# SBUF pools laid out so that the operands of every 512-column product start at multiples of 256 bytes

## Chip, cores and metric

The kernel runs on one core of a Trainium2 chip. The metric is the device time of one execution in microseconds (us); the time stated for a kernel is the median of its runs. TensorE's granted clock is given as a share of full speed: 1.00 is 2.4 GHz, 0.50 is 1.2 GHz.

## What is computed

One layer of a hybrid backbone over 2,048 latent tokens of width 1,024, with a prefix of 256 context tokens:

```
proj = rms_norm(x) * (1 + scale) + shift  @  w_in        # 2048 x 1024 @ 1024 x 5632, 11 slots of 512 channels
A: bidirectional gated recurrence (RG-LRU)      B: short gated convolution
C: GLU -> conv31 -> LayerNorm -> swish -> 512x512 product      D: 2-D box means minus the token
cat  = [ya*silu(za), yb*silu(zb), yc*silu(zc), yd*silu(zd)]        # 2048 x 2048
out  = rms_norm(x + gate * (cat @ w_out))                          # 2048 x 2048 @ 2048 x 1024
```

## The kernel before, in words

**The products.** Every float32 operand is split into a high and a low part (`split`, L104 to L107), and a product is three TensorE products into one PSUM bank: high by high, high by low, low by high. Almost all of TensorE's work is such products with a stationary operand (weights) of 128x128 and a moving operand of 128x512. The weights of each product are loaded anew (the profile's engine PEld), while the product before it still streams.

- The input projection (`project`, L331, its products at L339; `project_two`, L347, its products at L356): the moving operand is `hb`, the prepared tokens (four tiles of 32 KB per partition, pool `big`), the weights are `wh` and `wl` (pool `wp`), in two jobs also `whl` (pool `acc`). One `project` call is 2 x 8 x 3 x 2 = 96 products.
- The gates of group A (`lru_block`, L408): moving `xh`, `xl` (pool `lru`), weights `gwh`, `gwl` (pool `sm`).
- The pointwise product of group C (`finish_c`, L811): moving `uh`, `ul` (pool `mid`), weights `pw` (pool `lru`).
- The output projection (L992): a block scheme of seven 512-column products for each pair of token tiles, in the order 1, 2, 6, 7, 4, 5, 3. The moving operand is `wo` (pool `big`), the weights are `ahl` (pool `mid`, three buffers that take turns). 56 groups (7 blocks by 8 tiles) of 24 products each.
- Two smaller kinds with 256 columns: the modulation (`modulation_pair`, L226: moving `modwhl`, weights of only four columns) and the context's projection (`context`, L633: moving `hc`, weights `wh`, `wl`).

**The order.** The string `JOBS` (L37) orders the projections, mixers and gates by hand; within it a scheduler places each engine's instructions by priority. Evacuations of PSUM run at raised priority. Loads go through SP's queue, stores mostly through POOL's.

**Where tiles lie.** Pools lie one behind the other in SBUF in the order in which they are opened (L52 to L61): `const`, `big` (4 buffers), `mid` (3), `wst` (2), `wp` (3 for each of two tags), `lru` (4), `acc` (1), `zp` (3), `bp` (2), `sm`. A tag's buffer is as large as its largest tile, and each tile is rounded up to 32 bytes. All these are per partition. The compiled kernel before has these start addresses in bytes, and remainders by 256:

| tile (pool) | start of each buffer | remainder by 256 |
|---|---|---|
| `ident`, `onesm` (const) | 16,512; 17,024 | 128; 128 |
| `schl` (const) | 18,752 | 64 |
| `hb`, `wo`, `modwhl` (big) | 19,904 + 32,768 n | 192 |
| `ahl`, `uh`, `ul`, `hc` (mid) | 150,976; 159,296; 167,616 | 192; 64; 192 |
| `wh`, `wl` (wp) | 180,032 + 2,048 n | 64 |
| `xh`, `xl`, `pw` (lru) | 192,320 + 4,096 n | 64 |
| `whl`, `hl` (acc) | 208,704 | 64 |
| `gwh`, `gwl` (sm) | 223,776; 225,824 | 32 |

A mid buffer is 8,320 bytes because of its largest tile, `vc` (L492: two planes of 1,040 values); 8,320 is 32.5 x 256, so every second buffer has the other remainder. Within a tile the products' slices are steps of 512 or 2,048 bytes and change no remainder.

Of the kernel before, what the change touches and what calls it, by code (L numbers as in the profile page):

```python
# [8 lines left out]
F32 = mybir.dt.float32  # L9
F32R = mybir.dt.float32r  # L10
# [4 lines left out]
P = 128  # L15
T = 2048
# [3 lines left out]
NK = D // P  # L20
# [4 lines left out]
WINS = (2, 4, 8, 16)  # L25
# [19 lines left out]
def flow_backbone_kernel(  # L45
# [4 lines left out]
    nc = tc.nc  # L50
    PSUM = bass.MemoryType.PSUM
    const = ctx.enter_context(tc.tile_pool(name="const", bufs=1))  # L52
# [5 lines left out]
    acc_p = ctx.enter_context(tc.tile_pool(name="acc", bufs=1))  # L58
    zp = ctx.enter_context(tc.tile_pool(name="zp", bufs=3))
    bp = ctx.enter_context(tc.tile_pool(name="bp", bufs=2))  # L60
    sm = ctx.enter_context(tc.tile_pool(name="sm", bufs=2))  # L61
    dram = ctx.enter_context(tc.tile_pool(name="dram", bufs=1, space=bass.MemoryType.DRAM))
    pm = ctx.enter_context(tc.tile_pool(name="pm", bufs=4, space=PSUM))
# [17 lines left out]
    def z2(name, shape=(P, 512)):  # L81
        return zp.tile(list(shape), F32, tag="z2", name=name)

    def b2(name):
        return bp.tile([P, 512], F32, tag="b2", name=name)

    def mid_t(name, shape, dt=F32):
        return mid.tile(list(shape), dt, tag="mid", name=name)
# [7 lines left out]
    def gate_ps(name):  # L96
        return pg.tile([P, 512], F32, tag="pg", name=name)
# [6 lines left out]
    def split(hi, lo, src, sub=None):  # L104

        nc.scalar.activation(hi, src, AF.Copy)  # L106
        (sub or nc.vector).tensor_tensor(lo, src, hi.bitcast(F32), op=SUB)  # L107


    rows1 = z2("rows1", shape=(R_EARLY, W))  # L110
    for eng, r, n, src in (
        (nc.scalar, R_C, 2, c.rearrange("b (h w) -> (b h) w", w=W)),
# [27 lines left out]
        for kk in range(1, 4):  # L140
            load_modw(kk)

    ident = const.tile([P, P], F32, name="ident")
    with tc.high_priority(offset=3 * URGENT):
        make_identity(nc, ident)
    onesm = const.tile([P, P], F32R, name="onesm")
    nc.scalar.activation(onesm, ident, AF.Copy, bias=1.0 / W, scale=0.0)
    fixed = const.tile([P, 4], F32, name="fixed")
    ones2, eps_rms, eps_ln = fixed[:, 0:2], fixed[:, 2:3], fixed[:, 3:4]
# [1 line left out]
        nc.vector.memset(t, v)  # L151


    lacks = const.tile([P, sum(w // 2 for w in WINS)], F32, name="lacks")
    lack = []
    for w in WINS:
        at = sum(v // 2 for v in WINS if v < w)
# [7 lines left out]
    def par(r, q):  # L165
        return pt[:, q, r : r + 1]
# [210 lines left out]
        return gw  # L377

    def split_gate_weights(q):
        gh = sm.tile([P, 4, P], F32R, tag="gwh", name="gwh", bufs=1)  # L380
        gl = sm.tile([P, 4, P], F32R, tag="gwl", name="gwl", bufs=1)
        split(gh, gl, gate_weights(q))
        return gh, gl

# [101 lines left out]

    HP = T // 2 + 16

    def c_slots(q):
        v = mid_t("vc", (P, 2, HP))  # L492
        nc.gpsimd.memset(v[:, :, 0:8], 0.0)
        nc.gpsimd.memset(v[:, :, HP - 8 : HP], 0.0)

        def planes(b, ps):
            return v[:, :, 8 + 256 * b : 8 + 256 * (b + 1)], ps.rearrange("p (m e) -> p e m", e=2)

        def ev_g(b, ps):
            s, src = planes(b, ps)  # L500
            nc.scalar.activation(s, src, AF.Sigmoid)

        def ev_a(b, ps):
            s, src = planes(b, ps)
            nc.vector.tensor_tensor(s, src, s, op=MUL)

        return v, ev_g, ev_a

    def c_conv31(v, q):
        n = T // 2  # L510
        x1, x0 = v[:, 0, :], v[:, 1, :]
        even, odd = (lambda j: par(R_CCONV + 2 * j, q)), (lambda j: par(R_CCONV + 2 * j + 1, q))
        bb = aux["pool"].tile([P, n], F32, tag="conv", name="cb")
        nc.vector.tensor_scalar(bb, x1[:, 1 : 1 + n], odd(0), None, op0=MUL)
        for j in range(1, 15):
            nc.vector.scalar_tensor_tensor(bb, x1[:, 1 + j : 1 + j + n], odd(j), bb, op0=MUL, op1=ADD)  # L516

        nc.vector.tensor_tensor(x1, x1, x0, op=ADD)
        acc = acc_p.tile([P, n], F32, tag="acc", name="cacc")
        nc.vector.tensor_scalar(acc, x0[:, 0:n], even(0), None, op0=MUL)  # L520
        for j in range(1, 16):
            nc.vector.scalar_tensor_tensor(acc, x0[:, j : j + n], even(j), acc, op0=MUL, op1=ADD)  # L522

        end = sm.tile([P, 17], F32, tag="cend", name="cend", bufs=1)
        nc.vector.scalar_tensor_tensor(
            end[:, 1:17], x0[:, n : n + 16], 1.0, pt[:, q, R_CCONV : R_CCONV + 31 : 2], op0=MUL, op1=MUL, accum_out=end[:, 0:1]
        )

        nc.vector.tensor_tensor(x0[:, 0:n], acc, bb, op=ADD)
        nc.gpsimd.dma_start(u_d[q][:, 0, :], x0[:, 0:n])  # L530
        nc.vector.scalar_tensor_tensor(acc[:, : n - 1], x1[:, 1:n], csum[:, q, 0:1], acc[:, 1:n], op0=MUL, op1=SUB)
        nc.vector.scalar_tensor_tensor(
            acc[:, n - 1 : n], x1[:, n : n + 1], csum[:, q, 0:1], end[:, 0:1], op0=MUL, op1=SUB
        )
        for j in range(1, 16):
            nc.vector.scalar_tensor_tensor(acc, x1[:, 1 + j : 1 + j + n], csum[:, q, j : j + 1], acc, op0=MUL, op1=ADD)  # L536
        nc.vector.tensor_tensor(acc, acc, bb, op=SUB)
        nc.gpsimd.dma_start(u_d[q][:, 1, :], acc)
# [159 lines left out]
    def group_d(q):  # L698
        h = WINS[q] // 2
        g = mid_t("gd", (P, GR, GW))  # L700
        gf = g.rearrange("p r c -> p (r c)")

        def evac(b, ps):
            s = slice(512 * b, 512 * (b + 1))
            nc.scalar.activation(gf[:, s], ps, AF.Copy)
            if b % 2 == 1:
                s = slice(512 * (b - 1), 512 * (b + 1))
                nc.gpsimd.dma_start(dv_d[q][b // 2], gf[:, s])

        project(DV, q, evac)  # L710
        dw = sm.tile([P, P], F32, tag="dw", name="dw", bufs=1)
        nc.gpsimd.dma_start(dw, d_w[0, q])

        for rows, n in ((False, GW), (True, GR)):

            def cut(t, lo, hi):

                return t.rearrange("p r c -> p (r c)")[:, lo * GW : hi * GW] if rows else t[:, :, lo:hi]

            def back(t):  # L720

                return t[:, ::-1] if rows else t[:, :, ::-1]

            if h > 1:
                pre = acc_p.tile([P, h - 1, GW] if rows else [P, GR, h - 1], F32, tag="acc", name="pre")
                nc.vector.tensor_copy(cut(pre, 0, h - 1), cut(g, 0, h - 1))
                k = 1
                while k < h - 1:
                    upper = back(cut(pre, k, h - 1))
                    nc.vector.tensor_tensor(upper, upper, back(cut(pre, 0, h - 1 - k)), op=ADD)  # L730
                    k *= 2
            k = 1
            while k < h:
                nc.vector.tensor_tensor(cut(g, 0, n - k), cut(g, 0, n - k), cut(g, k, n), op=ADD)
                k *= 2
            upper = back(cut(g, h, n))
            nc.vector.tensor_tensor(upper, upper, back(cut(g, 0, n - h)), op=ADD)
            if h > 1:
                nc.vector.tensor_tensor(cut(g, 1, h), cut(g, 1, h), cut(pre, 0, h - 1), op=ADD)

            for lo, hi, f in ((0, h, lack[q]), (n - h + 1, n, lack[q][:, :0:-1])):
                if hi > lo:
                    m = hi - lo
                    ff = f.unsqueeze(2).broadcast_to([P, m, GW]) if rows else f.unsqueeze(1).broadcast_to([P, GR, m])
                    e = g[:, lo:hi, :] if rows else g[:, :, lo:hi]
                    nc.vector.tensor_tensor(e, e, ff, op=MUL)
        dbs = sm.tile([P, 1], F32, tag="dbs", name="dbs")
        nc.vector.tensor_tensor(dbs, par(R_DB, q), par(R_DSC, q), op=MUL)
        for b in range(NB):
            o, s = 512 * (b % 2), gf[:, 512 * b : 512 * (b + 1)]  # L750
            dv = b2("dvr")
            nc.sync.dma_start(dv, dv_d[q][b // 2][:, o : o + 512])
            nc.vector.scalar_tensor_tensor(s, s, 1.0 / (4 * h * h), dv, op0=MUL, op1=SUB)
            ps = gate_ps("dps")
            nc.tensor.matmul(ps, lhsT=dw, rhs=s, start=True, stop=True)  # L755
            nc.scalar.activation(s, ps, AF.Identity, bias=dbs, scale=par(R_DSC, q))
            nc.gpsimd.dma_start(y_d["d", q][b // 2][:, o : o + 512], s)
# [73 lines left out]


    def gate_mod(e):
        acc = sm.tile([P, P], F32, tag="macc", name="macc", bufs=1)
        mod_tile(2, e, 0, acc, [b2("mws").rearrange("p (k e) -> p k e", e=P) for _ in range(2)])
        mod_sums(2, e, 1, 0, acc)

# [22 lines left out]
    gcol = sm.tile([P, NK], F32, tag="gcol", name="gcol", bufs=1)  # L860
    nc.vector.tensor_copy(gcol, mod[:, 2, :, 0])
    nc.tensor.transpose(gps[:NK, :P], gcol, ident)
    grow = sm.tile([NK, P], F32, tag="grow", name="grow", bufs=1)
    nc.vector.tensor_copy(grow, gps[:NK, :P])
    gd = dram.tile([NK, P], F32, name="gd", tag="gd")
    nc.sync.dma_start(gd, grow)
# [183 lines left out]
```

## Time and profile before

| | |
|---|---|
| median of 3 runs | 1,550.73 us (1,548.19 to 1,552.17) |
| the profiled execution: its time | 1,551.9 us |
| the profiled execution: its span, first to last instruction | 1,549.8 us |
| granted clock of TensorE over the span | 0.985 |
| busy share: TensorE products, weight loads | 95%, 77% |
| busy share: VectorE, ScalarE, GpSimd | 72%, 43%, 11% |
| share of the chain that ended last: TensorE, "issue", DMA | 64%, 18%, 10% |

Busy time is a share of the span. Successive products overlap in the trace (one is shown as lasting some 390 ns, the next starts some 230 ns after it), so the distance between the starts of two products, here called the cadence, says what a product costs, not the duration shown.

### The profile page before, as it was taken

How to read it: one execution, taken by the hardware profiler on the slowest of the kernel's cores; microseconds unless marked ns; L12 is line 12 of the kernel's file. 1: busy time of each engine (PE TensorE's matmuls, PEld its weight loads, DVE VectorE, ACT ScalarE, POOL GpSimd, SP SyncE). 2: the span in 40 equal slices, each digit the busy share in tenths (PEclk: the TensorE clock that was granted, in tenths of full speed). 3: DMA queues.
4: the chain of work that ended last, by engine and by line, in shares of the span. 5: the costliest groups of instructions: out<-in, count | busy, mean ns of one | idle time of the engine just before them, and what ended most of it. 6: DMA issues, size and time to landing. Idle time of an engine off the chain costs nothing.

```text
span 1549.8 us, 17881 instructions
## 1 busy us (share of the span) xinstructions
PE 1479.4 (95%) x6457; PEld 1186.2 (77%) x6457; DVE 1117.4 (72%) x1573; ACT 662.4 (43%) x949; POOL 166.4 (11%) x290
## 2 busy tenths in 40 slices
PE   5999999999999999999999999979999699999997
PEld 3778888887788888788877887857877487788886
DVE  6889984859956898988754875554646446765897
ACT  7773475543144541244635435322424332433432
POOL 0200000100100000111011001313222210000000
PEclk9999999999999999999999999989999799999999
DMA  9412121322311223233253126557466977775674
GB/s 341 143 51 87 42 92 49 106 83 69 110 38 37 86 75 109 86 109 122 82 161 110 63 75 218 180 170 221 155 225 205 332 221 253 254 232 170 214 250 150
DMA packets 157308, 223.88 MB, mean 144 GB/s; under 512 B 16283, under 2 KB 98211, under 8 KB 157220
## 3 DMA queue, kind: packets, MB, share of 16 engines
q1 hardware_dynamic: 135836, 154.29, 31.4%
q0 software_dynamic: 19648, 65.31, 12.0%
q10 hardware_dynamic: 1736, 3.15, 0.7%
q8 instruction: 50, 0.82, 0.2%
q14 instruction: 38, 0.31, 0.1%
HBM read 149.29 MB, written 73.40 MB: 144 GB/s over the span
## 4 chain that ended last, share of the span: by engine, by line
PE 64%; issue 18%; DMA 10%; POOL 3%; DVE 3%; SPq 1%; ACT 1%; POOLq 0%; DVEq 0%; ACTq 0%
PE ps L339 45%; PE q L992 12%; PE gps L408 3%; PE ps L356 3%; DMA yp<-first 2%; DMA sums<-yp 1%; POOL sums L456 1%; DMA yt<-yb 1%; SPq L126 1%; DMA sums<-yt 1%; DMA wos<-in_w_out_dram 1%; DMA ws<-in_w_in_dram 1%; PE dps L755 1%; PE psc L633 1%; POOL second L452 1%
## 5 line engine op out<-in xcount | busy, mean ns | idle before, releaser
L339 PE MATMUL ps<-hb,wh 128*128 128x512 f32 x2560 | 730.1, 399 | 10.3 <-ACT sz L464 9.6
L339 PEld LDWEIGHTS ps<-hb,wh 128*128 128x128 f32 x2560 | 483.4, 189 | 131.4 <-ACT sz L464 11.4
L339 PE MATMUL ps<-hb,wl 128*128 128x512 f32 x1280 | 418.1, 398 | 0.0
L992 PE MATMUL q<-wo,ahl 128*128 128x512 f32 x1344 | 312.1, 394 | 14.2 <-ACT sz L464 10.1
L992 PEld LDWEIGHTS q<-wo,ahl 128*128 128x128 f32 x1344 | 253.4, 189 | 72.9 <-ACT sz L464 10.6
L339 PEld LDWEIGHTS ps<-hb,wl 128*128 128x128 f32 x1280 | 241.9, 189 | 58.8 <-issue 1.7
L106 ACT ACTIVATE wh<-ws 128x512 fp32r<-128x512 f32 x94 | 58.7, 627 | 174.3 <-PE ps L339 153.1
L470 DVE TENSOR_TENSOR sz<-sz,yt 128x512 f32<-128x512 f32 x48 | 32.9, 685 | 92.6 <-DMA yt<-yd 30.5
L107 DVE TENSOR_TENSOR wl<-ws,wh 128x512 fp32r<-128x512 f32 x91 | 62.1, 684 | 33.1 <-ACT wh L106 32.9
L464 ACT ACTIVATE sz<-ps 128x512 f32<-128x512 f32 x64 | 36.7, 595 | 102.3 <-DMA second<-sz 34.2
L536 DVE SCALAR_TENSOR_TENSOR cacc<-vc,csum,cacc 128x1024 f32<-128x1024 f32 x60 | 76.7, 1278 | 0.3
L522 DVE SCALAR_TENSOR_TENSOR cacc<-vc,pt,cacc 128x1024 f32<-128x1024 f32 x60 | 76.6, 1276 | 0.0
L414 ACT ACTIVATE gate<-gps,pt 128x512 f32<-128x512 f32 x64 | 40.9, 686 | 83.3 <-PE gps L408 83.2
L516 DVE SCALAR_TENSOR_TENSOR cb<-vc,pt,cb 128x1024 f32<-128x1024 f32 x56 | 71.7, 1281 | 0.0
L356 PE MATMUL ps<-hb,wh 128*128 128x512 f32 x192 | 65.6, 413 | 5.7 <-ACT sz L464 4.7
L106 ACT ACTIVATE wo<-wos 128x512 fp32r<-128x512 f32 x56 | 34.5, 628 | 74.4 <-DVE wos L910 42.5
L394 DVE SCALAR_TENSOR_TENSOR xc<-va,pt,xc 128x1024 f32<-128x1024 f32 x48 | 61.3, 1278 | 0.2
L423 DVE SCALAR_TENSOR_TENSOR xc<-xc,gate 128x1024 f32<-128x1024 f32 x16 | 19.6, 1224 | 44.5 <-ACT xc L422 44.5
L910 DVE TENSOR_TENSOR wos<-wos,wot 128x512 f32<-128x512 f32 x40 | 27.0, 689 | 33.8 <-DMA wos<-in_w_out_dram 18.4
L107 DVE TENSOR_TENSOR wo<-wos,wo 128x512 fp32r<-128x512 f32 x56 | 37.5, 687 | 18.1 <-ACT wo L106 17.4
L106 ACT ACTIVATE ahl<-s 128x1024 fp32r<-128x1024 f32 x32 | 33.5, 1054 | 36.4 <-PE q L992 32.9
L356 PEld LDWEIGHTS ps<-hb,wh 128*128 128x128 f32 x192 | 36.6, 194 | 15.3 <-ACT sz L464 5.9
(255 smaller groups left out, 1876.1 us busy)
## 6 DMA issues: line engine op xcount, KB each, us to landing
ws<-in_w_in_dram SPq DMA_DIRECT2D x96, 256.0 KB
s<-sums SPq DMA_DIRECT2D x32, 512.0 KB
wos<-in_w_out_dram SPq DMA_DIRECT2D x40, 256.0 KB
wot<-in_w_out_dram SPq DMA_DIRECT2D x40, 256.0 KB
modw<-in_mod_w_dram SPq DMA_DIRECT2D x8, 1024.0 KB
a<-second SPq DMA_DIRECT2D x16, 512.0 KB
xo<-in_x_dram SPq DMA_DIRECT2D x32, 256.0 KB
out_dram<-ys SPq DMA_DIRECT2D x32, 256.0 KB
```

Of the source, the lines that this page charges most:

```text
L106: nc.scalar.activation(hi, src, AF.Copy)
L107: (sub or nc.vector).tensor_tensor(lo, src, hi.bitcast(F32), op=SUB)
L339: nc.tensor.matmul(ps[u], lhsT=wk, rhs=hb[2 * pr + u][:, k, part, :], start=(k == 0 and n == 0), stop=(k == NK - 1 and n == 2),)
L356: nc.tensor.matmul(ps, lhsT=wk, rhs=hb[b][:, k, part, :], start=(k == 0 and n == 0), stop=(k == NK - 1 and n == 2),)
L394: nc.vector.scalar_tensor_tensor(xc, v[:, o + k : o + k + n], par(w0 + k, q), xc, op0=MUL, op1=ADD)
L408: nc.tensor.matmul(ps, lhsT=w[:, 2 * d + g, :], rhs=xx[:, u : u + m], start=(i == 0), stop=(i == len(terms) - 1))
L414: nc.scalar.activation(dst[:, u : u + m], ps, AF.Sigmoid, bias=par(bias, q))
L464: nc.scalar.activation(sz, ps, AF.Silu)
L516: nc.vector.scalar_tensor_tensor(bb, x1[:, 1 + j : 1 + j + n], odd(j), bb, op0=MUL, op1=ADD)
L522: nc.vector.scalar_tensor_tensor(acc, x0[:, j : j + n], even(j), acc, op0=MUL, op1=ADD)
L536: nc.vector.scalar_tensor_tensor(acc, x1[:, 1 + j : 1 + j + n], csum[:, q, j : j + 1], acc, op0=MUL, op1=ADD)
L992: nc.tensor.matmul(ps, lhsT=hl[:, a, k, :], rhs=wo[:, k, w, :], start=(k == 0 and e == 0), stop=(k == NK - 1 and e == 2))
```

## The change

The instructions and their order in the source stay; tiles move. (1) `lacks`, `ident` and `onesm` become the first tiles of `const`, and `lacks` grows from 15 to 32 values. (2) A new pool `gp` behind `bp` takes `gwh`, `gwl`, `dw`, and a tile `row` that serves both `macc` (in `gate_mod`) and, later, `grow`; they leave `sm`. (3) The two planes of `vc` grow from 1,040 to 1,056 values, which makes a mid buffer 8,448 bytes; the same eight values at each end are set to zero, and `c_conv31` works on the first 1,040.

```diff
@@ flow_backbone_kernel
+    gp = ctx.enter_context(tc.tile_pool(name="gp", bufs=1))
...
+    lacks = const.tile([P, 32], F32, name="lacks")
+    ident = const.tile([P, P], F32, name="ident")
+    onesm = const.tile([P, P], F32R, name="onesm")
...
-    ident = const.tile([P, P], F32, name="ident")
...
-    onesm = const.tile([P, P], F32R, name="onesm")
...
-    lacks = const.tile([P, sum(w // 2 for w in WINS)], F32, name="lacks")
@@ split_gate_weights
-        gh = sm.tile([P, 4, P], F32R, tag="gwh", name="gwh", bufs=1)
-        gl = sm.tile([P, 4, P], F32R, tag="gwl", name="gwl", bufs=1)
+        gh = gp.tile([P, 4, P], F32R, tag="gwh", name="gwh")
+        gl = gp.tile([P, 4, P], F32R, tag="gwl", name="gwl")
@@ c_slots
-    HP = T // 2 + 16
+    HP = T // 2 + 32
...
-        nc.gpsimd.memset(v[:, :, HP - 8 : HP], 0.0)
+        nc.gpsimd.memset(v[:, :, 8 + T // 2 : 16 + T // 2], 0.0)
@@ c_conv31
-        x1, x0 = v[:, 0, :], v[:, 1, :]
+        x1, x0 = v[:, 0, : n + 16], v[:, 1, : n + 16]
@@ group_d
-        dw = sm.tile([P, P], F32, tag="dw", name="dw", bufs=1)
+        dw = gp.tile([P, P], F32, tag="dw", name="dw")
@@ gate_mod
-        acc = sm.tile([P, P], F32, tag="macc", name="macc", bufs=1)
+        acc = gp.tile([P, P], F32, tag="row", name="macc")
@@ before the output projection
-    grow = sm.tile([NK, P], F32, tag="grow", name="grow", bufs=1)
+    grow = gp.tile([NK, P], F32, tag="row", name="grow")
```

## Rows read from the trace of the kernel before

**Rows 1.** The page's part 1: busy us, share of the span, instructions of each engine.

```profile
PE 1479.4 (95%) x6457; PEld 1186.2 (77%) x6457; DVE 1117.4 (72%) x1573; ACT 662.4 (43%) x949; POOL 166.4 (11%) x290
```

**Rows 2.** Busy time by stretch: length, each engine's busy us, clock, DMA share, GB/s.

```profile
127.00:1005.00 878.00, 877.31 (x3753) 704.00 (x3753) 673.36 (x849) 384.44 (x491) 83.12 (x157) 1.00 0.29 94
1005.00:1236.00 231.00, 200.02 (x799) 156.46 (x798) 123.84 (x197) 76.75 (x111) 58.66 (x81) 0.93 0.66 217
1236.00:1530.00 294.00, 290.63 (x1264) 236.57 (x1263) 205.81 (x306) 106.64 (x174) 11.34 (x18) 1.00 0.70 226
```

**Rows 3.** The chain that ended last, pieces at L339: start, length, products.

```profile
135.55 48.10 PE ps L339 x207
...
569.73 35.92 PE ps L339 x154
```

**Rows 4.** Busy time at L992 alone, four successive groups: length, PE, PEld, clock, DMA.

```profile
1244.32:1249.76 5.44, 5.44 (x25) 4.50 (x24) 1.00 0.43 112
1249.76:1255.35 5.59, 5.59 (x25) 4.52 (x24) 1.00 0.72 234
1255.35:1260.81 5.46, 5.46 (x26) 4.50 (x25) 1.00 0.81 239
1260.81:1266.25 5.44, 5.44 (x25) 4.50 (x24) 1.00 0.59 183
```

**Rows 5.** Groups by line and shape, TensorE: count, busy us, mean ns, idle before.

```profile
L339 PE MATMUL ps<-hb,wh 128*128 128x512 f32 x2560 | 730.1, 399 | 10.3 <-ACT sz L464 9.6 <-ACT vb L679 0.7
L339 PE MATMUL ps<-hb,wl 128*128 128x512 f32 x1280 | 418.1, 398 | 0.0
L992 PE MATMUL q<-wo,ahl 128*128 128x512 f32 x1344 | 312.1, 394 | 14.2 <-ACT sz L464 10.1 <-DVE ahl L107 3.1 <-ACT ys L998 0.7
L356 PE MATMUL ps<-hb,wh 128*128 128x512 f32 x192 | 65.6, 413 | 5.7 <-ACT sz L464 4.7 <-DVE hb L107 0.8
L811 PE MATMUL pwps<-uh,pw 128*128 128x512 f32 x128 | 41.1, 395 | 1.3 <-ACT uh L106 1.3
...
L408 PE MATMUL gps<-xl,gwh 128*128 128x512 f32 x64 | 25.3, 395 | 0.0
```

**Rows 6.** Busy time at L339 alone over the second stage: length, PE, PEld.

```profile
127.00:1005.00 878.00, 819.86 (x3428) 643.88 (x3429) 1.00 0.29 94
```

**Rows 7.** Timeline of PE at L339 while the granted clock was 0.50.

```profile
1020.00 1.05 PE L339 MATMUL ps<-hb,wh 128*128 128x512 f32 x2
1020.86 0.63 PE L339 MATMUL ps<-hb,wl 128*128 128x512 f32 x1
1021.28 1.05 PE L339 MATMUL ps<-hb,wh 128*128 128x512 f32 x2
```

**Rows 8.** Timeline of PE at L633, 256 columns, granted clock 1.00.

```profile
120.18 0.40 PE L633 MATMUL psc<-hc,wh 128*128 128x256 f32 x2
120.42 0.28 PE L633 MATMUL psc<-hc,wl 128*128 128x256 f32 x1
120.54 0.40 PE L633 MATMUL psc<-hc,wh 128*128 128x256 f32 x2
```

**Rows 9.** Busy time at L226 alone, 256 columns: length, PE, PEld, clock, DMA.

```profile
17.77:19.47 1.70, 1.70 (x17) 1.26 (x15) 1.00 1.09 348
```

**Rows 10.** Timeline of DVE, the low part of `ahl` in two successive buffers.

```profile
1404.56 1.23 DVE L107 TENSOR_TENSOR ahl<-a,ahl 128x1024 fp32r<-128x1024 f32 x1 [0.41 <-ACT ahl L106]
...
1410.15 1.23 DVE L107 TENSOR_TENSOR ahl<-a,ahl 128x1024 fp32r<-128x1024 f32 x1 [0.41 <-ACT ahl L106]
```

**Rows 11.** Busy time by stretch, all engines, the start and the fullest stretch of DVE.

```profile
0.00:50.00 50.00, 30.01 (x212) 21.52 (x213) 33.62 (x63) 37.53 (x65) 9.97 (x29) 1.00 0.89 299
500.00:600.00 100.00, 100.00 (x431) 80.48 (x430) 92.61 (x86) 45.60 (x55) 7.84 (x18) 1.00 0.24 79
```

**Rows 12.** The tiles `macc` and `grow`: durations min/median/max, first and last start.

```profile
L206 PE MATMUL modps<-fixed,macc x16: 165/210/251, 232.1 to 648.0; 128*128 128x2 f32 x16
...
L864 DVE COPY grow<-gateT x1: 272/272/272, 1202.1 to 1202.1; 8x128 f32<-8x128 f32 x1
```

## The prediction

> **What bounds the kernel.** The page's busy shares come first: TensorE is busy in 95% of the span and its weight loads in 77%, VectorE in 72% [rows 1]. The busy times by stretch say where that matters. From 127 to 1,005 us TensorE is busy in 877.3 of 878 us, so what its products cost is what the stage costs. From 1,005 to 1,236 it is busy in 200 of 231 and waits for others in between. From 1,236 to 1,530 it is busy in 290.6 of 294 [rows 2]. So for two stages of 1,172 us together the question is what one product costs.
>
> The chain of waits answers that for the input projection: 48.10 us for 207 products and 35.92 us for 154, together 84.02 us for 361, a cadence of 232.7 ns [rows 3]. The reader is to set beside this the output projection, where a group is 24 products of the same shape: 5.44 us (226.7 ns each), 5.59 us (232.9 ns), 5.46 us (227.5 ns), 5.44 us [rows 4]. The clock is 1.00 in all, the moving tile `wo` is the same, nothing waits (PE is busy throughout). What differs is the buffer of the weights. `ahl` takes the three mid buffers in turn, and the slow group is the one whose weights start at remainder 64 by 256; the others start at 192, as `wo` does. The input projection has weights at 64 and a moving operand at 192 throughout, and the cadence of the slow group. So the trace holds both cases: weights and moving operand at equal remainders, 226.7 ns; 128 bytes apart, 232.7 to 232.9.
>
> **What the change does to the addresses.** With `lacks` 128 bytes and first, `ident` starts at 16,640 = 65 x 256 and `onesm` at 17,152 = 67 x 256; the 32-byte roundings of the other tiles of `const` end it at 19,968 = 78 x 256, where `big` starts. `big` is 512 x 256 bytes, so `mid` starts at 151,040 = 590 x 256; its buffers are now 33 x 256, so all three have remainder 0. Everything behind them up to `gp` comes in multiples of 256. `gwh` and `gwl`, the only others, lie in `gp` and no longer in `sm`. So all operands of the 512-column products have remainder 0, equal for both. Remainder 0 itself occurs nowhere in the trace of before.
>
> **The sum, part by part.** A product that goes from unequal to equal remainders saves 232.7 - 226.7 = 6.0 ns, if 0 beside 0 does what 192 beside 192 does. I take that value because it is the only row with 512 columns and equal remainders. The products are 3,840 at L339, 1,344 at L992, 192 at L356 with two like rows of 96 beside it (384), 128 at L811 with 64 more (192), 64 at L408 with two like rows (192) [rows 5].
>
> - 127 to 1,005 us: 3,428 products of L339 [rows 6], all 192 of L408 and 48 of L811, 3,668 x 6.0 ns = 22.0 us. TensorE has no idle time here, so all of it lies on the path.
> - L992: 19 of the 56 groups read the middle buffer, 456 x 6.0 ns = 2.7 us; in the other groups nothing changes.
> - The rest: 412 of L339, 384 of L356, 144 of L811, 940 x 6.0 = 5.6 us. They lie where TensorE also waits for transfers and evacuations, so I count half, 2.8 us.
> - Sum 27.5 us.
>
> Bounds for one product, since remainder 0 is not in the trace. Below: while the clock was 0.50, three products took 1.28 us, 426.7 ns each [rows 7]; at 1.00 half of that is 213.3 ns, the 512 columns themselves, and there is nothing left to save beyond it. Above: at L633 a product of 256 columns with both operands at remainder 64, equal too, took 0.36 us / 3 = 120 ns [rows 8], and twice that is 240 ns for 512. At L226 256 columns with weights of only four columns took 1.70 us / 15 = 113.3 ns [rows 9], half of 226.7 to the digit. That speaks for 226.7 as what the moving operand needs at full clock by itself, with weights that don't get in its way, and so for the value that I take.
>
> A rule against the change: the Trainium skill, "TensorE: Matmul & The Clock Gate", section "Back-to-back issue gap", gives the gap as columns divided by 2.4 GHz plus 2.5 ns, with no term for an address. By it the change is worth 0. The trace disagrees: 226.7 and 232.9 for the same 512 columns [rows 4].
>
> What else the change could touch:
>
> - Other engines' instructions on moved tiles. The same instruction of VectorE on `ahl` takes 1.23 us in a buffer at remainder 192 and in one at 64 [rows 10]; nothing.
> - Loads. Their tiles now start elsewhere. The first 50 us are full of transfers, share 0.89 at 299 GB/s [rows 11], and the highest rate of a short stretch is 348 [rows 9]; if all went at that, 50 x (1 - 299/348) = 7 us would be saved at most. A loss has the same bound for want of a row. I take 0, since no row compares two remainders for a load.
> - The shared tile `row`: `grow` has to wait until `macc` was read last, at 648.0 us; it is written at 1,202.1 [rows 12]. Behind it on VectorE nothing is delayed. `gwh`, `gwl` and `dw` keep one buffer each in the new pool, so their waits stay.
> - The larger `vc`: the same columns are set to zero and added; nothing. No instruction and no DMA is moved past another by the source.
> - Cover that may go: VectorE is busy 92.6 of 100 us from 500 to 600 [rows 11]; with TensorE 2.6% faster that is 95%. PSUM evacuations queue there behind long convolution steps. If TensorE then meets a late one, part of that stage's gain is lost; some 0.5 us of 27.5, which I don't spell out further.
>
> So 1,551.9 - 27 = 1,525 us for the profiled execution. The median of the runs is 1.2 us below the profiled one; the forecast for the median is **1,524 us**.
>
> **The rivals.**
>
> - *More than equal remainders.* Starting at a multiple of 256 may also take away what 226.7 has over 213.3. At the lower bound, 3,668 x 19.4 = 71 us, the 1,344 of L992 from their mean of 228.9 (37 groups at 226.9, 19 at 232.9) x 15.6 = 21 us, half of 940 x 19.4 = 9 us: 101 us, 1,450. Halfway, at 220 ns, 3,668 x 12.7 + 1,344 x 8.9 + 470 x 12.7 = 47 + 12 + 6 = 65 us: **1,486**. For it: no operand then begins or ends inside a block of 256 bytes. Against: the 113.3 ns of rows 9, where the moving operand at 192 paid the same 6.25% over its 106.7 with hardly any weights to load; and VectorE would be at 98% in its fullest stretch, so that some would be lost.
> - *Nothing.* The two cadences may belong to the middle buffer for a reason other than its remainder, or TensorE may settle for 0 beside 0 in the pattern that it has for 192 beside 64. Then the time is that of before, **1,551**. For it: the rule above, and the fact that the trace has only three places of one tile to argue from. Against: `wh` and `wl` in other buffers at 64 show the slow cadence as well.
> - *Slower.* It is not equality that helps, but weights at 192, and 0 beside 0 settles like 64 beside 64 at L633, 120 ns for 256 columns [rows 8]: 240 ns for 512. Then 3,668 x 7.3 + 1,344 x 11.1 + 470 x 7.3 = 27 + 15 + 3 = 45 us more: **1,596**. The point from which this decides is a cadence c with 4,138 x (232.7 - c) = 1,344 x (c - 228.9), c = 231.8: above it the kernel is slower, because two thirds of the output projection already run at 226.8. For it: L633 is a case of equal remainders that is not fast. Against: at L992 equality was fast in 37 of 56 groups.
>
> **How the numbers follow.** The forecast has 0.58 and by itself a range of 1,515 to 1,535 (all or none of the half-counted products, the loads' 7 us, evacuations that come late). More than equality has 0.18, nothing 0.10, slower 0.12; the remaining 0.02 is a gain that is mostly given back on VectorE, about 1,540. The range takes in the forecast, nothing, and the larger half of the second case: 1,480 to 1,552; out of it lie the slower case (0.12) and the far end of more than equality (some 0.06). A difference of 0.3%, about 5 us, is what a measurement of this kernel can tell from none. Faster: 0.58 + 0.18 + 0.02 = 0.78; same 0.10; slower 0.12.
>
> **What would show it.** In the profile after, the chain's pieces at L339 should have 226.7 ns per product (207 in 46.9 us, not 48.1), all 56 groups of L992 should last 5.44 to 5.46 us, none 5.59, and the stretch that was 127 to 1,005 us should be some 22 us shorter with TensorE still busy throughout. Pieces at 216 to 220 ns would show the first rival, 5.59 in every group the second, 240 the third. If the cadence is 226.7 and the time hardly falls, look for new idle time of TensorE before L339, released by an evacuation on VectorE or ScalarE; if the time falls by more with the same cadence, look at the first 127 us. The prediction is wrong if a cadence other than 226 to 228 ns settles at L339.

## The result, and the profile after

The changed kernel takes 1,529.38 us (median of 4 runs, 1,526.85 to 1,531.54), the kernel before 1,549.67 us (4 runs): the ratio is 0.9867 with the interval 0.9845 to 0.9889, so 17 to 24 us are gone. The profiled execution took 1,526.85 us (span 1,524.9, granted clock 0.984 over the span) against 1,551.9 before, 25.05 us less. Lines of the kernel after stand 3 further down in the parts spoken of here: L342 is the input projection, L995 the output projection; the lines of `split` stand 1 further down (L107, L108).

The page's part 1 of the kernel after (busy us, share of the span, instructions), beside [rows 1]:

```profile
span 1524.9 us, 17881 instructions
...
PE 1453.0 (95%) x6457; PEld 1184.8 (78%) x6457; DVE 1116.2 (73%) x1573; ACT 662.1 (43%) x949; POOL 166.7 (11%) x290
```

The same 6,457 products keep TensorE busy for 26.4 us less. Nothing else changed its work: weight loads, VectorE, ScalarE and GpSimd are each within 1.4 us of before.

The page's groups by line, beside [rows 5] (count, busy us, mean ns, idle before):

```profile
L342 PE MATMUL ps<-hb,wh 128*128 128x512 f32 x2560 | 717.7, 395 | 11.5 <-ACT sz L467 10.8
...
L342 PE MATMUL ps<-hb,wl 128*128 128x512 f32 x1280 | 411.7, 393 | 0.0
L995 PE MATMUL q<-wo,ahl 128*128 128x512 f32 x1344 | 308.8, 391 | 15.8 <-ACT sz L467 10.0
```

Busy time falls by 12.4 and 6.4 us in the two groups of the input projection and by 3.3 us in the output projection. The idle time before L995 grows from 14.2 to 15.8 us.

Busy time by stretch, beside [rows 2 and 11] (length, each engine's busy us, clock, DMA share, GB/s):

```profile
0.00:50.00 50.00, 31.87 (x215) 22.69 (x216) 34.27 (x63) 37.54 (x65) 10.64 (x30) 1.00 0.83 300
126.02:985.72 859.70, 857.25 (x3753) 702.80 (x3753) 672.46 (x849) 384.19 (x491) 83.10 (x156) 1.00 0.29 96
```

The second row covers the products that lay between 127 and 1,005 us before. This long stage is bound by TensorE as before, but now 2.45 of its 860 us are idle, where 0.69 of 878 were. The first 50 us move 300 GB/s against 299, but with the DMA engines busy for 0.83 of the time instead of 0.89. Where transfers fill every engine, from 10 to 20 us, the same loads run at 393 GB/s instead of 371 (before, then after; the last two numbers are DMA share and GB/s):

```profile
10.00:20.00 10.00, 5.06 (x32) 3.11 (x32) 2.95 (x7) 9.94 (x25) 0.00 (x0) 1.00 1.06 371
10.00:20.00 10.00, 5.96 (x29) 3.46 (x30) 3.48 (x7) 9.94 (x25) 0.00 (x0) 1.00 1.06 393
```

The chain that ended last, two pieces at L342 (start, length, products), beside [rows 3]:

```profile
134.44 46.97 PE ps L342 x207
...
558.65 34.91 PE ps L342 x154
```

These are the same pieces as before, 46.97 us for 48.10 and 34.91 for 35.92: together 81.88 us for 361 products, 226.8 ns each where it was 232.7.

Busy time at L995 alone, three groups of 24 products in a row (length, PE, PEld, clock, DMA share, GB/s), beside [rows 4]:

```profile
1336.25:1341.69 5.44, 5.44 (x26) 4.51 (x24) 1.00 0.80 244
1341.69:1347.13 5.44, 5.44 (x26) 4.51 (x24) 1.00 0.51 162
1347.13:1352.57 5.44, 5.44 (x26) 4.51 (x24) 1.00 0.58 174
```

The group of 5.59 us, every third one before, is gone.

Where the 25 us lie can be read by numbering TensorE's products in both traces and subtracting the starts of equal numbers. The first product starts 0.6 us earlier; that at 127 us of before 1.0 us; that at 1,005 us 19.5 us; the first of the output projection (1,225 us) 23.4 us; the last 25.0 us. So the start gives 1.0 us, the long stage 18.5, the part between 3.9, and the output projection 1.6.

### The profile page after: what moved, and what is told of

It is laid out like the page before. It is cut to its first block, busy times and chain, and to the rows that moved or that the text cites. A ratio compares the mean times of both kernels' runs of the same rounds, so it can differ in the third digit from the quotient of the medians.

```text
span 1524.9 us, 17881 instructions
## 1 busy us (share of the span) xinstructions
PE 1453.0 (95%) x6457; PEld 1184.8 (78%) x6457; DVE 1116.2 (73%) x1573; ACT 662.1 (43%) x949; POOL 166.7 (11%) x290
## 4 chain that ended last, share of the span: by engine, by line
PE 63%; issue 17%; DMA 11%; POOL 3%; DVE 3%; SPq 1%; ACT 1%; POOLq 0%; DVEq 0%; ACTq 0%
PE ps L342 44%; PE q L995 12%; PE gps L411 3%; PE ps L359 2%; DMA yp<-first 2%; DMA sums<-yp 2%; DMA yt<-yb 2%; SPq L132 1%; POOL sums L459 1%; DMA wos<-in_w_out_dram 1%; DMA sums<-yt 1%; DMA ws<-in_w_in_dram 1%; PE dps L758 1%; PE psc L636 1%; DMA yt<-ya 1%
## 5 line engine op out<-in xcount | busy, mean ns | idle before, releaser
L342 PE MATMUL ps<-hb,wh 128*128 128x512 f32 x2560 | 717.7, 395 | 11.5 <-ACT sz L467 10.8
L342 PEld LDWEIGHTS ps<-hb,wh 128*128 128x128 f32 x2560 | 483.2, 189 | 119.5 <-ACT sz L467 13.0
L342 PE MATMUL ps<-hb,wl 128*128 128x512 f32 x1280 | 411.7, 393 | 0.0
L995 PE MATMUL q<-wo,ahl 128*128 128x512 f32 x1344 | 308.8, 391 | 15.8 <-ACT sz L467 10.0
L995 PEld LDWEIGHTS q<-wo,ahl 128*128 128x128 f32 x1344 | 252.6, 189 | 72.0 <-ACT sz L467 10.4
L342 PEld LDWEIGHTS ps<-hb,wl 128*128 128x128 f32 x1280 | 242.0, 189 | 52.2 <-issue 1.7
L107 ACT ACTIVATE wh<-ws 128x512 fp32r<-128x512 f32 x94 | 58.6, 626 | 159.7 <-PE ps L342 141.6
L108 DVE TENSOR_TENSOR wl<-ws,wh 128x512 fp32r<-128x512 f32 x91 | 62.1, 684 | 30.2 <-ACT wh L107 30.0
L359 PE MATMUL ps<-hb,wh 128*128 128x512 f32 x192 | 64.0, 405 | 4.9 <-ACT sz L467 4.0
L107 ACT ACTIVATE wo<-wos 128x512 fp32r<-128x512 f32 x56 | 34.5, 628 | 69.5 <-DVE wos L913 40.6
L108 DVE TENSOR_TENSOR wo<-wos,wo 128x512 fp32r<-128x512 f32 x56 | 37.3, 687 | 16.5 <-ACT wo L107 15.8
L107 ACT ACTIVATE ahl<-s 128x1024 fp32r<-128x1024 f32 x32 | 33.5, 1054 | 36.3 <-PE q L995 31.3
```

Source lines behind the costliest of these rows:

```text
L342: nc.tensor.matmul(ps[u], lhsT=wk, rhs=hb[2 * pr + u][:, k, part, :], start=(k == 0 and n == 0), stop=(k == NK - 1 and n == 2),)
L359: nc.tensor.matmul(ps, lhsT=wk, rhs=hb[b][:, k, part, :], start=(k == 0 and n == 0), stop=(k == NK - 1 and n == 2),)
L995: nc.tensor.matmul(ps, lhsT=hl[:, a, k, :], rhs=wo[:, k, w, :], start=(k == 0 and e == 0), stop=(k == NK - 1 and e == 2))
```

## The experiments

"Distance" below is the start of the weights less the start of the moving operand, in bytes, counted up to 256. The cadence is the mean over all pairs of products that follow one another at a line by less than 260 ns, or that of a group.

### All operands at remainder 64

The theory is that equality counts, its rival that the multiple of 256 does. A pad of 64 bytes at the head of `const` moves everything behind it alike.

```diff
+    const.tile([P, 16], F32, name="pad")
     lacks = const.tile([P, 32], F32, name="lacks")
```

> The changed kernel with 64 bytes more at the start of the first pool, so that every operand lies at remainder 64 by 256: equal, but not 0. Theory (only the distance between weights and moving operand counts): cadence 226.7 ns at the input and the output projection, time as the changed kernel, 1,525 to 1,532 us, ratio to the kernel before 0.985 to 0.989. Rival (the multiple of 256 counts): 233 to 240 ns as for operands at 64 in the kernel before, 1,550 us or more.

Measured: 1,531.04 us (median of 5 runs), before 1,551.36, ratio 0.9868 with 0.9849 to 0.9886. The chain's pieces:

```profile
135.20 46.97 PE ps L343 x207
...
559.49 34.91 PE ps L343 x154
```

They are the changed kernel's to 0.01 us, and the ratio is 0.9868 for 0.9867. With equal remainders the multiple of 256 adds nothing to a product. For the loads it does matter; here they run as in the kernel before:

```profile
10.00:20.00 10.00, 5.07 (x32) 3.08 (x32) 3.01 (x8) 9.94 (x25) 0.00 (x0) 1.00 1.06 370
```

The same stretch has 393 or 394 GB/s in the six kernels whose pool `big` starts at a multiple of 256 (the changed one, and the second to sixth experiment), and 370 to 377 in the five others.

### Distances of 64, 128 and 192

A larger `vc` makes the mid buffers 64 bytes longer by remainder: `ahl` takes distances 0, 64 and 128 in turn, and everything behind mid, the weights `wh` and `wl` too, lies at 192.

```diff
-    HP = T // 2 + 32
+    HP = T // 2 + 40
```

> The changed kernel with planes of 1,064 values in the largest mid tile: the three mid buffers lie at 0, 64 and 128, everything behind mid at 192. Theory: groups of the output projection, by their buffer, at 226.7 ns for a distance of 0, near 232.9 for 128, somewhere between for 64; the input projection, whose weights lie 192 behind, as slow as some unequal distance, 230 to 233 ns, so about 1,545 us. Rival (only the weights' own place counts, 192 good and 64 bad): input projection 226.7 ns, groups at 64 slow, at 0 and 128 unknown, about 1,530 us.

Measured (one run): 1,539.31 us. The chain at L342, then busy time at L995 for groups at distances 0, 64, 128 and 0:

```profile
134.46 47.39 PE ps L342 x207
```

```profile
1232.94:1238.38 5.44, 5.44 (x25) 4.50 (x24) 1.00 0.33 99
1238.38:1243.98 5.60, 5.60 (x25) 4.51 (x24) 1.00 0.63 198
1243.98:1249.56 5.58, 5.58 (x26) 4.52 (x24) 1.00 0.81 244
1249.56:1255.00 5.44, 5.44 (x26) 4.51 (x25) 1.00 0.74 213
```

Distances 64 and 128 cost nearly the same, 233.3 and 232.5 ns. But 192 is a middle case: 47.39 us / 207 = 228.9 ns. It is not just equal or unequal.

### Distances of 160, 64 and 224

```diff
-    HP = T // 2 + 32
+    HP = T // 2 + 20
```

> The changed kernel with planes of 1,044 values in the largest mid tile: the mid buffers lie at 0, 160 and 64, everything behind mid at 224. Theory: output projection at 226.7 ns in the first buffer, slower in the two others; input projection with a distance of 224 slower than 226.7, 230 to 233 ns, about 1,545 us. Rival (distances of a multiple of 64 matter, a distance of 32 more or less does not): input projection 226.7 ns.

Measured (one run): 1,553.45 us, as slow as before. `wh` and `wl` at 224:

```profile
136.69 48.30 PE ps L342 x207
```

That is 233.3 ns. So 192 was not the beginning of a return to equality, and the rival's 226.7 at 224 fell; the time is longer than the 1,545 us expected. The groups of the output projection in the buffers at 160 and 64 took 233.4 and 233.2 ns per product.

### The input projection's weights moved, the output projection's not

A pad of 128 bytes between mid and the pools behind it: the output projection keeps its equal remainders, the weights in `wp` go to distance 128, and the other pools behind mid move along.

```diff
     mid = ctx.enter_context(tc.tile_pool(name="mid", bufs=3))
+    pad = ctx.enter_context(tc.tile_pool(name="pad", bufs=1))
+    pad.tile([P, 32], F32, name="pad")
```

> The changed kernel with 128 bytes between mid and what lies behind it: weights of the input projection at 128, moving operand at 0; the output projection and the gates of group A stay at equal remainders. Theory: input projection back at 232.7 to 232.9 ns, output projection 226.7 ns, time 1,525 + 22 = 1,547 to 1,551 us. Rival (the change saves time elsewhere, in transfers or other engines): the time stays below 1,540 us although the cadence is slow.

Measured: 1,547.92 us (median of 12 runs), before 1,551.36, ratio 0.9981 with 0.9970 to 0.9993.

```profile
134.86 48.09 PE ps L344 x207
...
569.09 35.92 PE ps L344 x154
```

The pieces of before are back to 0.01 us, with every other part of the change in place; the cadence of the output projection stays at 226.9 ns. Nearly all of the gain goes with this one distance. The gates, whose remainders stay equal here, took 231.8 ns all the same, 226.9 in the changed kernel: they come 1 to 6 at a time between products of the input projection, which are 128 bytes apart.

### One kernel with 16 distances

Each group of the output projection takes its weights from a place within a longer `ahl` tile, 16 bytes further every three groups; the last eight groups are back at 0. The input projection is as in the changed kernel.

```diff
-            hl = mid_t("ahl", (P, 2, 8, P), F32R)
+            g = 8 * n + m
+            off = 4 * (g // 3) if g < 48 else 0
+            hl = mid_t("ahl", (P, 2112), F32R)[:, off : off + 2048].rearrange("p (a k t) -> p a k t", a=2, t=P)
```

> The changed kernel with the weights of the output projection put 16 bytes further for every three groups: 0, 16, 32 up to 240 bytes behind the moving operand, the last eight groups at 0 again. Theory (equal remainders are the one good case): 226.7 ns per product at 0, 229 to 234 at all others, so the projection takes some 1,344 x 4.5 ns = 6 us longer, 1,535 us. Rival (the fixed 13.3 ns over the bare columns are a meeting of the two reads as well, and some other distance avoids it): a cadence below 224 ns at one or more distances.

Measured (one run): 1,527.48 us. Busy time at this line (L997) for one group each at distances 16, 32, 96, 176, 192, 224, 240 and 0:

```profile
1225.44:1230.88 5.44, 5.44 (x25) 4.50 (x24) 1.00 0.64 194
1241.92:1247.53 5.61, 5.61 (x26) 4.51 (x25) 1.00 0.56 189
1311.59:1317.22 5.63, 5.63 (x26) 4.52 (x25) 1.00 0.69 242
1395.55:1401.07 5.52, 5.52 (x25) 4.50 (x24) 1.00 0.90 304
1412.08:1417.57 5.49, 5.49 (x25) 4.51 (x24) 1.00 0.68 200
1439.86:1445.47 5.61, 5.61 (x26) 4.50 (x25) 1.00 0.69 210
1462.12:1467.56 5.44, 5.44 (x25) 4.50 (x24) 1.00 0.66 186
1473.00:1478.44 5.44, 5.44 (x25) 4.50 (x24) 1.00 0.68 241
```

All 16, from the last of the three groups at each distance (mean from start to start, pairs under 260 ns):

| distance | 0, 16, 240 | 32, 48, 64 | 80 | 96 | 112 to 160 | 176 | 192 | 208, 224 |
|---|---|---|---|---|---|---|---|---|
| ns | 226.7 | 233.3 to 233.4 | 231.9 | 234.1 | 233.3 to 233.5 | 229.7 | 228.9 | 233.3 |

Three distances are fast, not one: 16 bytes to either side are as good as equality, 32 are not. 176 and 192 lie between, and nothing is below 226.7. The expected 1,535 us did not come: the total is 1.9 us under the changed kernel's median and 0.6 over its profiled run, though some 40 groups got slower by up to 0.19 us. Between the two profiled runs the pairs under 260 ns at this line add 6.1 us, and longer gaps give 4.0 back; the total of a single run did not show what the groups show.

### The output projection with two bytes per column

What is left of 226.7 over the 213.3 ns of 512 columns might be weights and moving operand meeting, or the width of the data. Here `wo` and `ahl` are bf16 instead of float32r, and the distances run as above. The high and low parts hold fewer bits; no product is left out.

```diff
-        t = big.tile([P, NK, 2, 512], F32R, tag="big", name=f"wo{i}")
+        t = big.tile([P, NK, 2, 512], BF, tag="big", name=f"wo{i}")
...
-            hl = mid_t("ahl", (P, 2, 8, P), F32R)
+            g = 8 * n + m
+            off = 8 * (g // 3) if g < 48 else 0
+            hl = mid_t("ahl", (P, 4224), BF)[:, off : off + 2048].rearrange("p (a k t) -> p a k t", a=2, t=P)
```

> As the sweep, but both operands of the output projection are kept as bfloat16 high and low parts, half the bytes per column, with the same steps of 16 bytes. This is another rounding of the split. Theory (226.7 ns is what reading four bytes per column takes, and the meeting with the weights comes on top): 214 to 216 ns per product at every distance, projection some 1,344 x 11 = 15 us shorter than in the changed kernel, 1,512 us. Rival (the 13.3 ns belong to the change of weights, whatever the bytes): 226.7 ns or more, and still a dependence on the distance.

Measured (one run): 1,516.93 us. Two groups at distance 128:

```profile
1339.48:1344.66 5.18, 5.18 (x25) 2.33 (x24) 1.00 0.57 185
1344.66:1349.84 5.18, 5.18 (x25) 2.33 (x24) 1.00 0.53 181
```

A group takes 5.18 us, 215.8 ns per product, here and, where nothing is waited for, at every other distance, and its weight loads are busy for 2.33 us instead of 4.5. The Trainium skill, "TensorE: Matmul & The Clock Gate", section "Back-to-back issue gap", gives for a single product columns divided by 2.4 GHz plus 2.5 ns, an estimate of 215.8 for 512. That agrees with this row, and not with any 512-column float32r row of this case at the full clock, 226.7 to 234.1.

### The kernel before plus 128 bytes

The pad of the fourth experiment, put into the kernel before: `wh` and `wl` go from remainder 64 to 192, where `hb` lies. Nothing starts at a multiple of 256.

> The kernel before with nothing but 128 bytes between mid and what lies behind it: weights of the input projection at 192 as their moving operand, nothing at a multiple of 256; in the output projection every third group stays slow, the gates of group A stay unequal. Theory: input projection 226.7 ns, output projection 5.44 and 5.59 us as before, time 22 to 23 us below before, about 1,528 to 1,532 us, ratio 0.985 to 0.988. Rival (the multiple of 256 does part of it): less than 15 us gained.

Measured: 1,532.05 us (median of 6 runs), before 1,548.9 (11 runs), ratio 0.9889 with 0.9869 to 0.9909.

```profile
134.02 46.97 PE ps L341 x207
...
559.41 34.94 PE ps L341 x154
```

One pad gives 16.9 us between the medians, less than the 22 to 23 expected, where the whole change gave 20.3, and the same chain to 0.03 us. Left behind are the middle `ahl` buffer (the mean cadence at that line is 229.2 ns, 226.9 in the changed kernel) and the gates' 512-column products (233.3 for 226.9).

### Two bytes per column everywhere

Both kernels with float32r replaced by bf16 in all split products (again fewer bits, nothing left out):

```diff
-F32R = mybir.dt.float32r
+F32R = mybir.dt.bfloat16
...
-        (sub or nc.vector).tensor_tensor(lo, src, hi.bitcast(F32), op=SUB)
+        (sub or nc.vector).tensor_tensor(lo, src, hi, op=SUB)
...
```

The changed kernel first:

> The changed kernel with bfloat16 high and low parts in place of float32r in every split product, so half the bytes per column everywhere. The parts hold fewer bits, so the products are rounded more coarsely; nothing is left out. Theory (the 11 ns over 215.8 are the four bytes per column): 215.8 ns at the input projection too, 3,840 x 11 + 1,344 x 11 = 57 us less than the changed kernel at most, with VectorE nearly full some 40 to 50 us, 1,480 to 1,490 us. Rival (VectorE or the transfers become the bound): cadence 215.8 with new idle time of TensorE, above 1,500 us.

Measured: 1,499.53 us (median of 4 runs), before 1,551.61, ratio 0.9664 with 0.9638 to 0.9690. Its busy shares, and the long stage (length, each engine's busy us, clock, DMA share, GB/s):

```profile
span 1494.6 us, 17748 instructions
...
PE 1383.5 (93%) x6334; PEld 643.4 (43%) x6457; DVE 1115.6 (75%) x1573; ACT 658.3 (44%) x949; POOL 165.1 (11%) x290
```

```profile
126.00:988.00 862.00, 833.97 (x3743) 380.46 (x3819) 684.56 (x869) 389.59 (x499) 88.98 (x162) 0.99 0.32 103
```

The cadence at L342 is 215.8 ns. TensorE's busy time falls by 69.5 us from the changed kernel (123 products are missing from this trace, so part of that is not real), the span by 30.3. In the long stage TensorE now idles for up to 28 us, where it was 2.45. The two largest waits of this stage (us in total, times, longest us):

```profile
PE ps L342 <- ACT sz L467: 6.0, 3, 2.3
PE modps L209 <- DVE macc L203: 4.6, 2, 3.3
```

The first are evacuations on ScalarE, 6.0 us in 3 waits. The clock fell as well: three stretches of this stage, 17 us together, ran at a granted clock of 0.50, two of them right behind waits of 3.3 us, and over the span it was 0.976 for 0.984. The time came out between the theory's and the rival's: cheaper products are partly given back where others become late.

Then the kernel before, with its operands 128 bytes apart:

> The same bfloat16 parts in the kernel before, with its addresses. Theory (the distance counts only where four bytes per column are read): the same cadence of 215.8 ns and the same time as the changed kernel with bfloat16, within 5 us. Rival (moving operand and weights still meet): some 20 us slower than that.

Measured: 1,495.39 us (median of 4 runs), ratio 0.9637 with 0.9611 to 0.9663.

```profile
PE 1382.5 (93%) x6334; PEld 644.5 (43%) x6457; DVE 1114.8 (75%) x1573; ACT 658.2 (44%) x949; POOL 165.1 (11%) x290
```

Its cadence is 215.8 ns too, and it is not slower than the one with equal remainders. With two bytes per column the change is worth nothing. This is the fastest kernel measured here, 3.6% under before, at the price of coarser split parts.

## Why the prediction was right

The forecast, a cadence of 226.7 ns wherever the remainders are equal, came about; 1,529.4 us were measured where 1,524 were predicted.

- *What bounds it, and what one product costs.* Right: TensorE stayed the bound of the long stage and the cadence went from 232.7 to 226.8 ns in the chain. That this comes from the distance between weights and moving operand is shown by moving the weights against the moving operand in both directions: the fourth experiment takes the gain back, the pad in the kernel before brings it. Both pads move the other pools behind mid too, but these hold no operand of L339.
- *0 beside 0 does what 192 beside 192 does.* Right, and 64 beside 64 does it too. The reading of equality as the only good case was too narrow: ±16 bytes do as well, and 176 and 192 are middle cases.
- *The sum.* 27.5 us were predicted for the profiled execution, 25.05 measured. The long stage gave 18.5 instead of 22.0: the saving is 5.8 ns per product in the mean of the whole line (232.8 to 227.0) rather than 6.0, some 21.0 us over the products that follow one another by less than 260 ns, and the longer gaps took back 2.5 us. Of these, 1.8 us are idle time that was not there before:

```profile
PE dps L758 <- issue: 1.1, 1, 1.1
PE ps L342 <- ACT sz L467: 0.7, 1, 0.7
```

Only the second, a late evacuation, is the cover that the prediction thought might go and put at 0.5 us, and it came on ScalarE, not on VectorE; the first is one pause before the product of the box means, for which the profile shows no wait. The part between gave 3.9 for 2.8. The output projection gave 1.6 for 2.7. Its products did save (3.3 us of busy time), but it now waits more often for the split of `ahl` on VectorE, as this line of PE's waits after shows (us in total, times, longest us); before it was 3.1 us [rows 5]:

```profile
PE q L995 <- DVE ahl L108: 5.1, 5, 3.0
```

- *The start.* Taken as 0 for want of a row; now rows show that the loads do run faster, 393 GB/s for 371 from 10 to 20 us. The first product, which waits for the load of `rows` (7.6 us, 8.1 before), starts at 7.6 to 7.7 us in the six kernels with `big` at a multiple of 256 and at 8.1 to 8.2 in the five others. What this is worth further on is not shown: the product at 127 us of before starts between 124.4 and 128.2 us in the six, and in the others within these bounds. So the 1.0 us is not shown to come from the change. The bound of 7 us held.
- *The median.* The profiled execution of the kernel after is the fastest of its four runs, that of before lay 2.2 us above the median. So the medians show 20.3 us rather than 25, and most of the 5.4 us between forecast and result is this. The step that set the median 1.2 us under the profiled time did not carry over.
- *More than equal remainders* (1,486) fell: 226.7 ns is the least of all 16 distances with four bytes per column at the full clock. The argument for it, a stretch over 213.3 ns that might go, was sound in one respect only: that stretch does go, to 215.8, with two bytes per column, whatever the address.
- *Nothing* and *slower* fell. The row that the slower rival rested on, 120 ns for 256 columns at equal remainders [rows 8], has not changed by being put at 0 beside 0:

```profile
119.13 0.40 PE L636 MATMUL psc<-hc,wh 128*128 128x256 f32 x2
119.37 0.28 PE L636 MATMUL psc<-hc,wl 128*128 128x256 f32 x1
119.49 0.40 PE L636 MATMUL psc<-hc,wh 128*128 128x256 f32 x2
```

Three products in 0.36 us, as before. So 256 columns between full weight loads are no guide to 512; the 113.3 ns with four columns of weights [rows 9] were.

For 256 columns the distance does not count in the same way. In the fourth experiment they are 128 bytes apart, and three of them take 0.36 us in the lines below, 118.2 ns each in the mean at the full clock, where the changed kernel has 119.4 with equal remainders:

```profile
120.50 0.40 PE L638 MATMUL psc<-hc,wh 128*128 128x256 f32 x2
...
120.86 0.40 PE L638 MATMUL psc<-hc,wh 128*128 128x256 f32 x2
```

What stays open is why the distances from 32 to 224 are slow, and 176 and 192 less so. That weight loads and the moving stream meet in reading would fit a dependence on the distance and its end when the loads are busy for half the time (2.33 for 4.5 us), but no run here shows such a meeting. The products at half the clock limit this reading: in the kernel before, 128 bytes apart and at a granted clock of 0.50, a weight load is shown as 0.33 us of the 0.43 that each product takes,

```profile
1020.43 0.33 PEld L339 LDWEIGHTS ps<-hb,wl 128*128 128x128 f32 x1
```

and yet three products take 1.28 us [rows 7], 426.7 ns each, the same as in the changed kernel at that clock with equal remainders:

```profile
1000.29 1.05 PE L342 MATMUL ps<-hb,wh 128*128 128x512 f32 x2
...
1001.57 1.05 PE L342 MATMUL ps<-hb,wh 128*128 128x512 f32 x2
```

So at that clock the distance costs nothing. Distances that are no multiple of 16 were not tried.

## What to carry to other kernels

Where TensorE is the bound and reads float32r at the full clock, look at the start addresses of weights and moving operand by 256 bytes: equal remainders, or 16 bytes apart, saved 2.6% of each 512-column product here, and one pad of 128 bytes between two pools got most of it. A ring of buffers whose size is no multiple of 256 shows it by itself, as a cadence that changes with the buffer; measure from start to start, because the durations shown overlap. Then see which engine is late next before counting the gain in full. The faster loads went with a start at a multiple of 256 itself, not with a distance.

## What the hardware showed that was not expected

- The cost goes by the distance and not steadily: 226.7 ns from -16 to +16 bytes, 228.9 at 192, 229.7 at 176, 231.9 to 234.1 elsewhere. To the last ns it is not the distance alone: 128 bytes cost 232.5 ns in the second experiment, 232.8 at the input projection before and 233.5 in the sweep, and products with equal remainders, a few at a time between others 128 bytes apart, cost 231.8 (the gates of the fourth).
- At a granted clock of 0.50 the same products take 426.7 ns whether the operands are 0 or 128 bytes apart.
- Loads into SBUF ran at 393 to 394 GB/s, from 10 to 20 us, with the pool `big` at a multiple of 256 and at 370 to 377 with it 64, 128 or 192 bytes beyond one; a packet of 1,024 bytes took 51 ns before and 46 ns after, in the median.
- With bf16 the same 512 columns take 215.8 ns at every distance tried, and a weight load is shown as 98 ns instead of 188: the 6,457 loads are busy for 643.4 us, not 1,184.8.
